# Two 512-token tiles of two batch rows, interleaved through every layer of a two-layer hybrid block, with a byte ring of 1 MB weight units

## The chip, the cores and the metric

The kernel runs on all eight cores of one Trainium2 chip (two dies, cores 0 to 3 and 4 to 7). The cores do not communicate: each works on two of the sixteen batch rows, with its own copy of all weights in memory. The metric is the device time of the slowest core in microseconds (us), one launch, everything included: the cast of the f32 weights, the conditioning and the whole sequence.

Executions come in two states. In the fast one all eight cores agree within about 1% (13215.8 to 13330.1 us in the profile of the kernel before). In the slow one the cores of one die, sometimes of both, show a lower granted TensorE clock and the time is longer: in one slow run of experiment 1, cores 4 to 7 took 13351 to 13659 us at 0.84 to 0.85, cores 0 to 3 12495 to 12507 at 0.93.

## The reference, cut to what matters

Two layers; 2048 channels; each core has 2 rows of 2048 tokens, that is 8 tiles of 512 tokens.

```
for l in range(2):
    mod = silu(c) @ w_mod[l] + b_mod[l]                  # 2048 x 12288, once per batch row
    sh_m, sc_m, g_m, sh_f, sc_f, g_f = split(mod, 6)
    h = x * (1 + sc_m) + sh_m
    a, val, gate, z = split(h @ w_in[l])                 # 2048 -> 3584
    y = concat(pool(a),                                  # trailing means, carry 16 tokens
               silu(LN(depthwise_conv31(val * sigmoid(gate)))),   # carries 31 tokens
               u * (tril(w_sgu) @ LN(v)))                # u, v = split(gelu(z)), chunks of 128
    x = LN(alpha * x + g_m * (y @ w_out[l]))             # 2048 -> 2048
    h = x * (1 + sc_f) + sh_f
    x = LN(alpha * x + g_f * (relu(h @ w_ff1[l])**2 @ w_ff2[l]))  # 2048 -> 8192 -> 2048
```

What matters: nothing in a tile can go on across an LN until the LN is done, and a tile needs only the tail of the tile before it *in the same row* (16 tokens for pooling, 31 for the convolution). Two tiles of different rows are independent.

## The kernel before

The activations are kept with channels on partitions, so an LN sums over partitions. TensorE does that with a matrix of ones. Weights arrive in slots of 2.1 MB (128 partitions x 8192 bf16), three slots deep. The first tile casts each slot from f32 on GpSimd's queue and stores the bf16 copy back to memory; later tiles read the copy.

```python
def w_issue():
    ...
    rb_ = WR[i % 3]
    if i < NSLOT * len(layers):                       # first tile
        k.dma("pool", rb_.v(BF16), wsl_d[rows, :], [], [rb_.reg], ...)      # cast
        k.dma("sp", wbfull_d[rows, :], rb_.v(BF16), [rb_.reg], [R_slot[g]], ...)  # store, if nt > 1
    else:
        k.dma("sp", rb_.v(BF16), wbfull_d[rows, :], [R_slot[g]], [rb_.reg], ...)
```

The modulation matrix is loaded whole (48 slots) before any tile starts:

```python
for grp in range(NGC // 4):                           # 48 times, 2.1 MB each
    k.dma("pool", wb_.v(BF16), wmod_d[grp * 128:(grp + 1) * 128, :], ...)   # cast
    for kc in range(KC):
        ... nc.tensor.matmul(bank[0:2, :], lhsT=c2v[:, kc, :], rhs=wv[:, kc * 512:(kc + 1) * 512], ...)
```

After each output chunk, GpSimd makes a bf16 copy and a bf16 square, and TensorE adds both up over partitions. After the last chunk the norm runs as one block:

```python
def resid_evac(l, b, gidx, oc, bank, bankr, pend):
    ... vector.scalar_tensor_tensor(out=xT[:, oc, :], in0=bank, scalar=gate, in1=xT[:, oc, :], ...)
    ... gpsimd.tensor_copy(out=rb[:, i, :], in_=xT[:, oc, :])
    ... gpsimd.tensor_tensor(out=rsq[:, i, :], in0=xT[:, oc, :], in1=xT[:, oc, :], op=ALU.mult)
    def stats():
        ... tensor.matmul(banks[SUMB], lhsT=oneb, rhs=rb[:, i, :], start=(oc == 0), stop=(oc == KC - 1))
        ... tensor.matmul(banks[SQB], lhsT=oneb, rhs=rsq[:, i, :], start=(oc == 0), stop=(oc == KC - 1))
    ...

def main_ln(...):
    ...                                               # flush stats, then mean and 1/std
    for kc in range(KC):
        ...                                           # VectorE: subtract mean; multiply by 1/std
        ...                                           # ScalarE: h chunk for the next stage; new x chunk
```

The stages of one tile follow one another in program order, one tile after the other:

```python
for ti in range(nt):                                  # 8 tiles
    ...                                               # load x, transpose on TensorE
    for li, l in enumerate(layers):
        ...                                           # input projection, conv, gating, output, norm,
        ...                                           # first MLP matmul, second, norm
    ...                                               # transpose, store y
```

The convolution multiplies by 31 diagonal matrices per 128 channels, which GpSimd builds anew for each tile and layer.

Of the kernel before, what the change touches and what calls it, by code (L numbers as in the profile page):

```python
# [19 lines left out]
NSLOT = 44  # L20
SLOTE = 8192
# [4 lines left out]
NGC = 192  # L26

# [28 lines left out]
class K:  # L56
    def __init__(self, nc, es):
        self.nc, self.es = nc, es
        self.eng = {}
        for name, h in (("pe", nc.tensor), ("act", nc.scalar), ("dve", nc.vector),  # L60
                        ("pool", nc.gpsimd), ("sp", nc.sync)):
            self.eng[name] = Eng(h, self.newsem("e_" + name), is_pe=(name == "pe"))
# [29 lines left out]
    def op(self, eng, fn, reads=(), writes=(), inc=True):  # L92
        E = self.eng[eng]
        self._waits(E, reads, writes)
        ins = fn()
        v = E.sem.count + 1
        if inc:
            ins.then_inc(E.sem.h, 1)
            E.sem.count += 1
        for R in reads:  # L100
            if R.r.get(E.sem, 0) < v:
                R.r[E.sem] = v
        for R in writes:
            R.w = (E.sem, v)
            R.r = {}
        return ins

    def dma(self, q, out, in_, reads, writes, sem, **kw):
        E = self.eng[q]
# [9 lines left out]
        return ins  # L119

# [18 lines left out]
def build_program(nt, layers, stop_after=None):  # L139
    n_cores, gather = 1, False  # L140
    nc = bass.Bass("TRN2", target_bir_lowering=False)
    ntok = nt * T
    nloc_slots = (L_ALL * NSLOT) // n_cores
    nloc_gc = NGC // n_cores
    nloc_grp = nloc_gc // 4
# [3 lines left out]
    x_d = dram("x", [ntok, D], F32, "ExternalInput")  # L149
    y_d = dram("y", [ntok, D], F32, "ExternalOutput")  # L150
    wsl_d = dram("wsl", [nloc_slots * 128, SLOTE], F32, "ExternalInput")
    wmod_d = dram("wmod", [NGC // 4 * 128, 8192], F32, "ExternalInput")
    bmod_d = dram("bmod", [128, NGC], F32, "ExternalInput")
    c2_d = dram("c2", [128, 32], F32, "ExternalInput")
    NPP = L_ALL * (6 * 31 + 6 * 3 + 4 + 16 * 4)
    pp_d = dram("pp", [128, NPP], F32, "ExternalInput")
    sgb_d = dram("sgb", [1, L_ALL * 2 * 768], F32, "ExternalInput")
    bsr_d = dram("bsr", [1, L_ALL * 6 * 128], F32, "ExternalInput")
    wp_d = dram("wp", [128, L_ALL * 4 * 128], F32, "ExternalInput")
    wst_d = dram("wst", [128, L_ALL * 6 * 128], F32, "ExternalInput")  # L160
    wbfull_d = dram("wbfull", [L_ALL * NSLOT * 128, SLOTE], BF16, "Internal")
    wbsh_d = wbfull_d
# [3 lines left out]
    with es:  # L166
        k = K(nc, es)
        ARENA = 212800
        arena_t = es.enter_context(nc.sbuf_tensor("arena", [128, ARENA], U8))
        arena = arena_t[:, :]  # L170
        psum_t = es.enter_context(nc.psum_tensor("ps", [128, 8 * 512], F32))
        psum = psum_t[:, :]
        banks = [psum[:, i * 512:(i + 1) * 512] for i in range(8)]
        bank_r = [Region("ps", i * 2048, (i + 1) * 2048, f"bank{i}") for i in range(8)]
        rr = [0]

        def nextbank():
            i = rr[0] % 6
            rr[0] += 1
            return banks[i], bank_r[i]  # L180
        SUMB, SQB = 6, 7

        cur = [0]

        def alloc(name, nbytes, at=None):
            if at is None:
                lo = (cur[0] + 63) // 64 * 64
                cur[0] = lo + nbytes
                assert cur[0] <= ARENA, (name, cur[0])
            else:  # L190
                lo = at
            return Buf(arena, lo, nbytes, name)

        XT = alloc("xT", 32768)
        HT = alloc("hT", 16384)
        U0 = (cur[0] + 63) // 64 * 64
        cur[0] = U0 + 65536
        WR = [alloc(f"wr{i}", 16384) for i in range(3)]
# [7 lines left out]
        YT = ualloc("yT", 16384)  # L206
        AT = ualloc("aT", 4 * 528 * 4)
        HC = ualloc("hcT", 6 * 544 * 2)
        CV = ualloc("cvT", 6 * 512 * 2)
        UT = ualloc("uT", 6 * 512 * 2)  # L210
        VLN = ualloc("vln", 4 * 768 * 2)
        VG = ualloc("vg", 768 * 4)
        PT = ualloc("ptmp", 2 * 528 * 4)
        DG = ualloc("diag", 31 * 128 * 2)
        H1 = Buf(arena, U0, 65536, "h1T")
        DG2 = Buf(arena, AT.lo, 31 * 128 * 2, "diag2")
        STG = [Buf(arena, U0 + i * 8192, 8192, f"stg{i}") for i in range(2)]
        WMB = [Buf(arena, U0 + i * 16384, 16384, f"wmb{i}") for i in range(4)]
        MF = Buf(arena, XT.lo, NGC * 16 * 4, "mf")
        WP32 = Buf(arena, XT.lo + 12288, L_ALL * 4 * 128 * 4, "wp32")  # L220
        WST32 = Buf(arena, XT.lo + 16384, L_ALL * 6 * 128 * 4, "wst32")
        ONESF = Buf(arena, XT.lo + 22528, 512, "onesf")
        IOTA = Buf(arena, XT.lo + 23040, 64, "iota")
        IOTF = Buf(arena, XT.lo + 23104, 64, "iotf")
        MSEL = Buf(arena, XT.lo + 23168, NGC * 16 * 4, "msel")
        RB = alloc("rb", 3 * 1024)
        RSQ = alloc("rsq", 3 * 1024)
        MEAN = alloc("mean", 2048)
        RSTD = alloc("rstd", 2048)
        TMPA = alloc("tmpa", 2048)  # L230
        FT = alloc("ft", 2 * 2048)
        SQT = alloc("sqt", 2 * 1024)
        ID32 = alloc("id32", 512)
        IDB = alloc("idb", 256)
        ONEB = alloc("oneb", 256)
        ONER = alloc("oner", 512)
        WMT = alloc("wmt", L_ALL * 6 * 128 * 2)
        WPB = alloc("wpb", L_ALL * 4 * 128 * 2)
        SGG = alloc("sgg", L_ALL * 768 * 4)
        SGBB = alloc("sgbb", L_ALL * 768 * 2)  # L240
        SGB32 = Buf(arena, XT.lo + 40960, L_ALL * 768 * 4, "sgb32")
        BSR = alloc("bsr", L_ALL * 6 * 128 * 4)
        PP = alloc("pp", NPP * 4)
        MOD2 = alloc("mod2", NGC * 2 * 4)
        DER = alloc("der", 9 * L_ALL * 32 * 4)
        INVC = alloc("invc", 4 * 16 * 4)
        AHALO = alloc("ahalo", L_ALL * 4 * 16 * 4)
        HHALO = alloc("hhalo", L_ALL * 6 * 32 * 2)
        SMALL = alloc("small", 256)
        CACT = Buf(arena, XT.lo + 36864, 256 * 4, "cact")  # L250
        SEL = Buf(arena, XT.lo + 39552, 32 * 4, "sel")
        EPSB = alloc("eps", 16)
        if nloc_gc <= 32:
            MODL = Buf(arena, XT.lo + 37888, nloc_gc * 16 * 4, "modl")
            BMOD = Buf(arena, XT.lo + 39424, nloc_gc * 4, "bmod")
        else:
            MODL = Buf(arena, WR[0].lo, NGC * 16 * 4, "modl")
            BMOD = Buf(arena, WR[1].lo, NGC * 4, "bmod")
# [3 lines left out]
        for nm, n in (("convw", 6 * 31), ("convb", 6), ("lncg", 6), ("lncb", 6), ("ls", 4),  # L262
                      ("lnmg", 16), ("lnmb", 16), ("lnfg", 16), ("lnfb", 16)):
            ppo[nm] = (o, n)
            o += L_ALL * n
        assert o == NPP

        def ppv(nm, l, i0=0, n=1):
            o, per = ppo[nm]
            a = o + l * per + i0  # L270
            return PP.v(F32)[:, a:a + n]

        csem = k.newsem("csem")
        castsem = k.newsem("castsem")
        gsem = k.newsem("gsem")
        msem = k.newsem("msem")
        wmsem = [k.newsem(f"wmsem{i}") for i in range(4)]
        ringsem = [k.newsem(f"ring{i}") for i in range(3)]
        stgsem = [k.newsem(f"stgs{i}") for i in range(2)]
        osem = [k.newsem(f"osem{i}") for i in range(2)]  # L280

        R_wbsh = Region("d_wbsh", 0, 1, "wbsh")
        R_wbfull = Region("d_wbfull", 0, 1, "wbfull") if gather else R_wbsh
        R_modsh = Region("d_modsh", 0, 1, "modsh")
        R_modfull = Region("d_modfull", 0, 1, "modfull") if gather else R_modsh
        R_y = Region("d_y", 0, 1, "y")

        C2 = Buf(arena, XT.lo + 36864, 32 * 4, "c2")
        BMD = Buf(arena, XT.lo + 37888, NGC * 4, "bmd")
        for buf, src in ((PP, pp_d), (C2, c2_d), (BMD, bmod_d), (WP32, wp_d), (WST32, wst_d)):  # L290
            k.dma("sp", buf.v(F32), src, [], [buf.reg], csem)
        k.dma("sp", BSR.v(F32), bsr_d.partition_broadcast(128), [], [BSR.reg], csem)
        k.dma("sp", SGG.v(F32), sgb_d[:, 0:L_ALL * 768].partition_broadcast(128), [], [SGG.reg], csem)
        k.dma("sp", SGB32.v(F32), sgb_d[:, L_ALL * 768:2 * L_ALL * 768].partition_broadcast(128), [], [SGB32.reg], csem)
        for b_ in (PP, C2, BMD, WP32, WST32, BSR, SGG, SGB32):
            b_.reg.w = (csem, csem.count)

        R_slot = {g: Region("d_wb", g, g + 1, f"wb{g}") for g in range(L_ALL * NSLOT)}
        stsem = [k.newsem(f"wst{i}") for i in range(3)]
        ringsem_sw = [k.newsem(f"ringsw{i}") for i in range(3)]  # L300

        k.op("dve", lambda: nc.vector.memset(EPSB.v(F32)[:, 0:1], EPS), [], [EPSB.reg])
        k.op("dve", lambda: nc.vector.memset(EPSB.v(F32)[:, 1:2], EPSM), [EPSB.reg], [EPSB.reg])
        k.op("pool", lambda: nc.gpsimd.memset(ONESF.v(F32), 1.0), [], [ONESF.reg])
        k.op("pool", lambda: nc.gpsimd.memset(ONEB.v(BF16), 1.0), [], [ONEB.reg])
        k.op("pool", lambda: nc.gpsimd.memset(ONER.v(F32), 1.0), [], [ONER.reg])
# [624 lines left out]
```

## Time and profile before

| | kernel before |
|---|---|
| median of three runs | 13378.98 us (13274.98 to 14025.92; the last is a slow run) |
| span in the profile | 13330.1 us |
| TensorE busy | 11420.8 us, 86% |
| VectorE, ScalarE, GpSimd busy | 21%, 17%, 12% |
| until the first tile starts | 770 us |
| first tile | 1870 us |
| a steady tile | 1518 us |

The last three rows come from the timeline and the table of windows. In all views of the profile PE is TensorE, PEld its weight loads, DVE VectorE, ACT ScalarE, POOL GpSimd and SP the engine that issues the plain weight transfers; L781 is line 781 of the kernel; `arena<-x` is a tile written from another. In a list of waits, `PE ps L550 <- DMA arena<-x` says that PE, at L550 and writing `ps`, waited for the DMA that writes `arena` from `x`. `ps` is TensorE's output memory, `arena` the one on-chip tensor that holds all buffers, `wsl` and `wmod` the f32 layer weights and modulation matrix, `wbfull` (`wb` in the new kernel) the bf16 copy of the weights in memory.

The page's chain of work that ended last, by engine, says the same in one line (shares of the span):

```profile
PE 74%; DMA 12%; DVE 6%; issue 5%; ACT 3%; POOL 0%; another core or an unknown queue 0%; DVEq 0%; ACTq 0%; SPq 0%; POOLq 0%
```

A quarter of the path is not TensorE: 12% are transfers (for the most part the modulation and the first tile), and 9% are VectorE and ScalarE, which come onto the path mainly in the norms and the modulation next to them, though each is busy for just a fifth of the time. The slices, the waits, the stage rows and the timeline across a norm stand in the prediction.

### The profile page before, as it was taken

To read this page: it belongs to the slowest core of one execution; us is meant where nothing else is said; L and a number is where in the kernel's file an instruction comes from. 1 tells how busy PE (TensorE), PEld (TensorE's weight loads), DVE (VectorE), ACT (ScalarE), POOL (GpSimd) and SP (SyncE) were. 2 spreads that over 40 slices of the span, in tenths; PEclk is the share of its full clock that TensorE was granted. 3 is DMA by queue.
4 is the path that set the end of the run, shared out by engine and by line. 5 is a ranking of instruction groups with operands and counts; after the bars stand their busy time and mean duration, and the time that the engine had idled before them with its cause. 6 is when DMAs were issued, how large, how long until landed. Compare 5 with 4: busy or idle time off the path is not lost.

```text
span 13330.1 us, 133467 instructions; the slowest of 8 cores (13215.8 to 13330.1 us)
## 1 busy us (share of the span) xinstructions
PE 11420.8 (86%) x51360; PEld 5122.7 (38%) x51360; DVE 2806.1 (21%) x4092; ACT 2329.1 (17%) x3346; POOL 1598.7 (12%) x1333
## 2 busy tenths in 40 slices
PE   3468878789898998989898898979898898979898
PEld 1133333334344443434344343434344343434433
DVE  0012031131312212131222212131221213122221
ACT  0011021120312212120212212031211212021220
POOL 0011120020201001020201101020100102020100
PEclk7679989899898999999999999989999999989987
DMA  8889989824243332334233232324233332433332
GB/s 138 141 187 199 215 191 209 201 111 149 96 151 126 127 139 108 137 116 150 104 144 140 108 139 108 145 108 152 108 139 139 112 135 110 149 114 139 120 120 101
DMA packets 184169, 1841.38 MB, mean 138 GB/s; under 512 B 14720, under 2 KB 14848, under 8 KB 85248
## 3 DMA queue, kind: packets, MB, share of 16 engines
q1 hardware_dynamic: 107136, 1514.06, 30.6%
q0 software_dynamic: 71808, 285.22, 13.5%
q10 hardware_dynamic: 4608, 33.56, 0.6%
q8 instruction: 426, 6.98, 0.2%
q14 instruction: 191, 1.56, 0.0%
HBM read 1899.89 MB, written 218.10 MB: 159 GB/s over the span
## 4 chain that ended last, share of the span: by engine, by line
PE 74%; DMA 12%; DVE 6%; issue 5%; ACT 3%; POOL 0%; another core or an unknown queue 0%; DVEq 0%; ACTq 0%; SPq 0%; POOLq 0%
PE ps L781 25%; PE ps L771 23%; PE ps L615 8%; PE ps L738 7%; DMA arena<-wsl 7%; PE ps L674 5%; DMA arena<-wmod 4%; DVE arena L504 3%; PE ps L578 2%; DMA y<-arena 1%; PE ps L340 1%; DMA arena<-x 1%; PE ps L528 1%; ACT arena L561 1%; PE ps L531 1%
## 5 line engine op out<-in xcount | busy, mean ns | idle before, releaser
L781 PE MATMUL ps<-arena 128*128 128x512 bf16 x16384 | 3662.9, 386 | 117.0 <-DMA arena<-wsl 117.0
L771 PE MATMUL ps<-arena 128*128 128x512 bf16 x15360 | 3376.3, 383 | 84.6 <-DMA arena<-wsl 84.6
L781 PEld LDWEIGHTS ps<-arena 128*128 128x128 bf16 x16384 | 1622.1, 99 | 2125.7 <-issue 345.0
L771 PEld LDWEIGHTS ps<-arena 128*128 128x128 bf16 x15360 | 1514.4, 99 | 1943.8 <-issue 206.5
L518 DVE SCALAR_TENSOR_TENSOR arena<-ps,arena 128x512 f32<-128x512 f32 x512 | 384.6, 751 | 4439.2 <-PE ps L781 3634.6
L747 DVE SCALAR_TENSOR_TENSOR arena<-ps,arena 128x512 bf16<-128x512 f32 x1024 | 705.6, 692 | 2865.2 <-ACT arena L745 2865.0
L738 PE MATMUL ps<-arena 128*128 128x512 bf16 x4096 | 1017.5, 397 | 314.5 <-ACT arena L724 231.1
L523 POOL CAST arena<-arena 128x512 bf16<-128x512 f32 x512 | 312.0, 609 | 8037.1 <-DVE arena L518 8037.1
L615 PE MATMUL ps<-arena 128*128 128x512 bf16 x5632 | 1233.2, 382 | 34.1 <-DMA arena<-wsl 34.1
L745 ACT ACTIVATE arena<-ps 128x512 f32<-128x512 f32 x1024 | 610.4, 598 | 2866.4 <-PE ps L771 2857.9
L615 PEld LDWEIGHTS ps<-arena 128*128 128x128 bf16 x5632 | 553.2, 98 | 709.7 <-issue 58.0
L738 PEld LDWEIGHTS ps<-arena 128*128 128x128 bf16 x4096 | 409.3, 100 | 881.4 <-issue 450.2
L668 POOL TENSOR_TENSOR arena<-arena 128x3968 bf16<-128x3968 bf16 x96 | 654.0, 6820 | 707.4 <-DVE arena L646 470.0
L494 ACT ACTIVATE arena<-arena 128x512 f32<-128x512 f32 x48 | 34.7, 723 | 3902.2 <-DVE arena L491 3901.8
L674 PE MATMUL ps<-arena 128*128 128x512 bf16 x2976 | 656.5, 379 | 0.0
L578 PE MATMUL ps<-arena 128*128 128x384 bf16 x2048 | 433.4, 358 | 239.0 <-ACT arena L510 202.3
L340 PE MATMUL ps<-arena 128*2 128x512 bf16 x768 | 270.9, 530 | 391.3 <-DMA arena<-wmod 391.3
L524 POOL TENSOR_TENSOR arena<-arena 128x512 bf16<-128x512 f32 x512 | 531.5, 1038 | 0.0
L760 PE MATMUL ps<-arena 128*128 128x512 bf16 x1024 | 285.8, 411 | 271.2 <-ACT arena L510 271.0
L513 ACT ACTIVATE arena<-arena 128x512 f32<-128x512 f32 x512 | 418.2, 817 | 145.1 <-DVE arena L507 109.3
L674 PEld LDWEIGHTS ps<-arena 128*128 128x128 bf16 x2976 | 290.0, 98 | 355.7 <-issue 7.7
L578 PEld LDWEIGHTS ps<-arena 128*128 128x128 bf16 x2048 | 210.0, 103 | 460.8 <-issue 354.8
(103 smaller groups left out, 4503.1 us busy)
## 6 DMA issues: line engine op xcount, KB each, us to landing
arena<-wbfull SPq DMA_DIRECT2D x616, 2048.0 KB, 7.8
arena<-wsl POOLq DMA_DIRECT2D x88, 2048.0 KB, 40.0
wbfull<-arena SPq DMA_DIRECT2D x88, 2048.0 KB, 14.8
arena<-wmod POOLq DMA_DIRECT2D x48, 2048.0 KB, 34.1
arena<-x SPq DMA_DIRECT2D x32, 1024.0 KB, 4.9
y<-arena ACTq DMA_DIRECT2D x32, 1024.0 KB, 4.3
arena<-sgb SPq DMA_DIRECT2D x2, 768.0 KB, 14.8
arena<-wst SPq DMA_DIRECT2D x1, 768.0 KB, 9.4
```

Of the source, the lines that this page charges most:

```text
L340: k.op("pe", lambda kc=kc, wv=wv, bank=bank: nc.tensor.matmul(bank[0:2, :], lhsT=c2v[:, kc, :], rhs=wv[:, kc * 512:(kc + 1) * 512], start= ...
L513: k.op("act", lambda kc=kc: nc.scalar.activation(out=xT[:, kc, :], in_=xT[:, kc, :], func=AF.Identity, scale=ppv(gname, l, kc), bias=ppv(b ...
L524: k.op("pool", lambda: nc.gpsimd.tensor_tensor(out=rsq[:, i, :], in0=xT[:, oc, :], in1=xT[:, oc, :], op=ALU.mult), [xr(oc)], [rsr])
L578: k.op("pe", lambda kc=kc, wv=wv, bank=bank, tb=tb: nc.tensor.matmul(bank[:, 0:384], lhsT=hT[:, kc, tb * 128:(tb + 1) * 128], rhs=wv[:, kc ...
L615: k.op("pe", lambda kc=kc, e0=e0, wv=wv, bank=bank: nc.tensor.matmul(bank, lhsT=wv[:, e0:e0 + 128], rhs=hT[:, kc, :], start=(kc == 0), sto ...
L668: k.op("pool", lambda c=c, diag=diag: nc.gpsimd.tensor_tensor(out=diag, in0=idb.unsqueeze(1).to_broadcast([128, 31, 128]), in1=ppv("convw" ...
L674: k.op("pe", lambda c=c, kk=kk, bank=bank, diag=diag: nc.tensor.matmul(bank, lhsT=diag[:, kk, :], rhs=hcT[:, c, 32 - kk:544 - kk], start=( ...
L738: k.op("pe", lambda kc=kc, ki=ki, e0=e0, wv=wv, bank=bank: nc.tensor.matmul(bank, lhsT=wv[:, e0:e0 + 128], rhs=yT[:, kc, :], start=(ki == ...
L745: k.op("act", lambda: nc.scalar.activation(out=ft[:, j % 2, :], in_=bank, func=AF.Square), [bankr], [fr])
L747: k.op("dve", lambda: nc.vector.scalar_tensor_tensor(out=h1T[:, j, :], in0=bank, scalar=0.0, in1=ft[:, j % 2, :], op0=ALU.is_gt, op1=ALU.m ...
L771: k.op("pe", lambda kc=kc, e0=e0, wv=wv, bank=bank: nc.tensor.matmul(bank, lhsT=wv[:, e0:e0 + 128], rhs=hT[:, kc, :], start=(kc == 0), sto ...
L781: k.op("pe", lambda j=j, wv=wv, bank=bank: nc.tensor.matmul(bank, lhsT=wv[:, j * 128:(j + 1) * 128], rhs=h1T[:, j, :], start=(j == 0), sto ...
```

## The change

The intent: give TensorE work of another tile while one tile's norm runs, and spread the modulation matrix over the first pair's stages. The tiles of the two batch rows form a pair, and a pair goes through each stage as A, B, with everything that is not the stage's own matmuls placed between its steps as background items. Buffers had to shrink for a second tile's x: weights come in units of 1.05 MB (128 x 4096 bf16) in a ring of 40960 bytes per partition (five units). The core of the diff (cuts marked):

```diff
-NSLOT = 44
-SLOTE = 8192
+UE = 4096
+RING = 40960
...
+class Bg:
+    def pump(self, i):
+        want = len(self.items) * (i + 1 - self.s0) / float(self.s1 - self.s0)
+        while self.done < len(self.items) and self.done < want:
+            self.items[self.done]()
+            self.done += 1
...
-    nc = bass.Bass("TRN2", target_bir_lowering=False)
+    nc = bass.Bass("TRN2", target_bir_lowering=False, dynamic_dma_scratch_size=4096)
-        ARENA = 212800
+        ARENA = 225088
-        XT = alloc("xT", 32768)
+        X = [alloc("xA", 32768), alloc("xB", 32768)]
-        WR = [alloc(f"wr{i}", 16384) for i in range(3)]
+        RG = alloc("ring", RING)
...
+        def ring_fill():
+            while ring["issued"] < len(order):
+                ...                                   # next unit's bytes lo .. lo + n
+                if any(a < lo + n and lo < b_ for _, a, b_ in ring["live"]):
+                    return
+                ...                                   # cast, cast + store, or read, as before
...
 # statistics (in resid)
-            k.op("pool", lambda: nc.gpsimd.tensor_copy(out=rb[:, i, :], in_=xT[:, oc, :]), [xr(oc)], [rbr])
-            k.op("pool", lambda: nc.gpsimd.tensor_tensor(out=rsq[:, i, :], ..., op=ALU.mult), ...)
-            ...                                       # two bf16 matmuls with ones per chunk
+            k.op("act", lambda: nc.scalar.activation(out=sq[i], in_=xT[b][:, oc, :], func=AF.Square), ...)
+            k.op("pool", lambda: nc.gpsimd.tensor_tensor(out=acc, in0=p0, in1=xT[b][:, oc, :], op=ALU.add), ...)
+            k.op("pool", lambda: nc.gpsimd.tensor_tensor(out=acq, in0=q0, in1=sq[i], op=ALU.add), ...)
+            # two f32 matmuls with ones per norm, in ln_stats_items
...
 # schedule
-        for ti in range(nt):
-            ...
+            for u in range(16):
+                mod_unit(u)                           # 16 of 96 modulation units first
+            ...
+                    bgs = [Bg(pool_items(1, l, first), 7, 20), Bg(conv_ln_items(0, l, SQ, sq), 0, 7)]
+                    if start:
+                        bgs.append(Bg(mod_items(range(16, 40)), 0, 17))
+                    run(in_steps(1, l, first), bgs)
+                    ...
+                    run(out_steps(0, l), [Bg(conv_ln_items(1, l, FT, ft), 0, 12)])
+                    bgs = [Bg(main_ln_items(0, l, "lnmg", "lnmb", h_items(0, l, S1F, SHF)), 0, 15)]
+                    ...
+                    run(out_steps(1, l), bgs)
+                    run(ff1_steps(0, l), [Bg(main_ln_items(1, l, "lnmg", "lnmb"), 0, 50)])
+                    run(ff2_steps(0, l), [Bg(h_items(1, l, S1F, SHF), 0, 32)])
+                    ...
+                    run(ff1_steps(1, l), bgs)         # A's second norm beside B's MLP
```

`run(steps, bgs)` issues one step (usually 16 matmuls), then as many background items as are due. Three smaller things go with it: the convolution's diagonal matrices are now six weight units a layer, made on the host; the gating unit's LN gain and bias are folded into one multiply-add after its matmul; and the modulation matmuls have the weights stationary, with two moving columns.

## The prediction

> **What bounds the kernel now.** I first read the busy shares and the slices of the page. TensorE (PE) is busy 11420.8 us of a 13330.1 us span; no other engine exceeds 21%. In the slices the first row is PE, the second the granted PE clock, the third the DMA engines:
>
> ```profile
> PE   3468878789898998989898898979898898979898
> PEclk7679989899898999999999999989999999989987
> DMA  8889989824243332334233232324233332433332
> ```
>
> There are three stages: two slices with PE near half idle (the modulation matrix is loaded), then about six with the DMA engines at 80 to 90% or more (the first tile, whose weights are cast from f32 and stored back as bf16), then a steady part with DMA at 20 to 40% and PE near full, with dips. Next I asked for what PE waits for (us in total, times, longest):
>
> ```profile
> PE ps L340 <- DMA arena<-wmod: 391.3, 48, 43.1
> PE ps L760 <- ACT arena L510: 271.0, 219, 10.0
> PE ps L738 <- ACT arena L724: 231.1, 80, 10.8
> PE ps L578 <- ACT arena L510: 202.3, 128, 8.4
> PE ps L793 <- ACT arena L513: 179.2, 128, 8.3
> PE ps L550 <- DMA arena<-x: 147.7, 29, 14.7
> PE ps L781 <- DMA arena<-wsl: 117.0, 32, 5.4
> PE ps L771 <- DMA arena<-wsl: 84.6, 22, 5.8
> ```
>
> The four rows on ACT are one thing: a layer norm stands between two matmul stages of the only tile there is, so PE waits for statistics, normalisation and the affine step. Then the stage table (busy us of each engine, then clock, DMA share, GB/s), one row for the first tile and one for a steady tile, and the timeline of PE around a norm and inside a dense stage:
>
> ```profile
> 770.00:2640.00 1870.00, 1472.41 (x6287) 641.86 (x6287) 352.99 (x523) 287.41 (x412) 249.78 (x233) 0.89 0.92 203
> 8718.00:10236.00 1518.00, 1364.42 (x6275) 618.35 (x6273) 348.47 (x503) 287.41 (x412) 186.60 (x148) 0.94 0.34 128
> ```
>
> ```profile
> 8220.11 207.36 PE L771 MATMUL ps<-arena 128*128 128x512 bf16 x960
> ...
> 9438.54 0.38 PE L531 MATMUL ps<-arena 128*128 128x512 bf16 x1 [0.62 <-POOL arena L524]
> 9447.21 0.48 PE L578 MATMUL ps<-arena 128*128 128x384 bf16 x1 [8.29 <-ACT arena L510]
> 9448.72 0.48 PE L578 MATMUL ps<-arena 128*128 128x384 bf16 x1 [1.03 <-ACT arena L510]
> ```
>
> The dense stage runs at 207.36/960 = 216 ns a matmul. Across the norm PE stands 8.29 us and then goes at the pace of the normalisation. So the steady part is bound by PE plus exposed norms, and the first tile by DMA.
>
> [...] the dense stretches have 1.00, a steady tile with its norms 0.94. [...] eight cores run the same dense stages at 1.00. [...] (core 1, then core 2, same stretch):
>
> ```profile
> 12960.00:13020.00 60.00, 60.00 (x230) 24.81 (x229) 7.61 (x11) 6.58 (x11) 0.00 (x0) 0.81 0.29 106
> 12960.00:13020.00 60.00, 60.00 (x280) 27.20 (x279) 12.16 (x18) 10.15 (x17) 0.00 (x0) 1.00 0.41 146
> ```
>
> [...] the f32 weights come on the POOL queue alone, the bf16 ones on SP's. [...]
>
> **Cost of a megabyte.** From the queue table:
>
> ```profile
> q1 hardware_dynamic: 107136, 1514.06, 30.6%
> q0 software_dynamic: 71808, 285.22, 13.5%
> ```
>
> q1: 0.306 x 13330 / 1514 = 2.7 us per MB of bf16. q0: 0.135 x 13330 / 285 = 6.3 us per MB delivered by a cast. A cast with its store, when that is all there is, from the first tile's timeline:
>
> ```profile
> 2470.93 15.66 PE L781 MATMUL ps<-arena 128*128 128x512 bf16 x64 [3.98 <-DMA arena<-wsl]
> 2490.75 15.66 PE L781 MATMUL ps<-arena 128*128 128x512 bf16 x64 [3.73 <-DMA arena<-wsl]
> ```
>
> 19.8 us for 2.1 MB, 9.4 us per MB. The modulation casts alone come four (8.4 MB) in 61 us: 7.3 us per MB.
>
> **The change, part by part.** PE work of one layer of one tile now: 512-wide matmuls 352 (input) + 4 + 186 (convolution) + 12 + 256 (output) + 2048 (MLP) + 64 (norm statistics) = 2922 at 216 ns = 631 us; 128 of 384 columns at 0.16 us = 21; together with the small ones about 653 us. Two layers and 128 transposes at about 0.15 us: 1325 us. The steady tile takes 1518, so about 193 us are lost to norms, x and y traffic and a cold clock.
>
> *Statistics.* The 64 statistics matmuls (13.8 us) go; VectorE, ScalarE and GpSimd sum over channels, and 4 f32 matmuls remain [...]. New minimum about 642 us per layer and tile. GpSimd adds twice per output chunk, 2 x 1.04 us (the row of L524), within the 3.45 us that 16 matmuls take; ScalarE and VectorE also stay below a step's time. The convolution's diagonal matrices no longer cost GpSimd 654 us; they come as 6 more units a layer.
>
> *Interleaving.* Each norm, modulation, x load and y store of one tile is now placed between matmul steps of the other. A pair has four layer-tiles: 4 x 642 = 2569, plus 256 transposes 36, plus what I leave exposed: about 20 for x and y staging (one buffer, and the x loads queue behind weight loads on SP), about 12 per layer where a norm's end and the next stage meet (24), and 10 for clock dips. 2660 us a pair against 3036 now, 376 less, three times: 7980 us. Weights are still read for each tile: 96.5 MB a layer x 2.7 = 260 us of DMA beside 642 of PE, so hidden.
>
> *First pair.* Tile A casts and stores, tile B reads back, and 80 of 96 modulation units (84 MB) now travel with layer 0. By stage, max of PE and DMA. Layer 0: input A 14.7 MB x 9.4 = 137; convolution A 59; input B 97 PE + 46 for modulation matmuls, against 40 + 25 MB x 7 = 216 of DMA, so 216; convolution B 41; output 78 and 81; MLP A twice 33.5 x 9.4 = 313; MLP B twice 270. Sum 1778. Layer 1, without modulation: 137 + 59 + 97 + 41 + 78 + 56 + 313 + 313 + 221 + 221 = 1536. Together 3314; five units of prefetch carry some slack from PE-bound into DMA-bound stages, so I take 3250. Modulation matmuls: 32 a unit at 62 ns (24 small ones took 1.50 us), 2 us, 96 times.
>
> *Start and end.* Now PE gets the first x at 766 us. Then only 16 modulation units come first: 16.8 MB x 7.3 = 123, plus x and constants: 150. The last tile's norm and store stay exposed: 50.
>
> Sum: 150 + 3250 + 7980 + 50 = **11430 us**. Against today's 13330: start 770 to 150, first two tiles 1870 + 1518 to 3250, three pairs 9108 to 7980.
>
> **The rivals.** *The clock becomes the bound.* With no dips PE runs dense for milliseconds, where now 440 us is the longest stretch. [...] For it: those rows, and one of three runs 5% slower. Against it: 1.00 in every other dense stage of all cores. I give lasting throttling 5 to 10%, occasional throttling (up to 700 us) another 20%.
>
> *DMA holds the first pair longer.* [...] stores on SP wait for casts, and reads and x loads stand behind them; a cast on POOL waits for PE and the store, and the norm sums stand behind it. The ring is 5 MB where it was 6, and z units cut it. If casts reach only 80% of today's rate, the first pair costs 500 more: 11900. Against it: the first tile now keeps the DMA engines at 0.92 with a similar depth.
>
> *The norm is only moved.* If the GpSimd sums lag, or ScalarE's table switches pile up, PE waits at each new statistics matmul; 5 us at 28 places would add 140. *Transfers are not the steady bound*: a share of 0.34 speaks against it.
>
> **Range and chances.** I add 90 for some throttling to 11430: 11520. Low side, 11200: more slack carried, or stalls nearly nil. High side, 12150: a throttled stretch, or slow casts with some throttling. Only lasting throttling brings it near 13379.
>
> **What would show it.** Modulation waits ahead of the first input matmul down from about 770 to about 150 us; the first pair ending near 3400, DMA share near 0.9 in it and PE waiting for wsl; a steady pair near 2660 with clock 0.98 or more and the waits on the norm's ACT rows nearly gone; statistics matmuls waiting under 2 us. Wrong would be: 0.81 over whole slices, DMA waits in the steady pairs, or GpSimd ahead of PE.

**What the sum came to.** The sum, 150 + 3250 + 7980 + 50 = 11430 us, contains two things:

- *The f32 statistics matmuls*, four per layer and tile, at 0.9 us each: 3.6 of the 642 us, 14 of a pair's 2660, 43 of the 7980. The trace before has no f32 matmul of 512 columns, so nothing there showed the figure. In the kernel after, two of them take 0.86 us inside a dense stretch (L558, 5056.93 to 5057.79 us), 0.43 each.
- *The allowances*: 20 for x and y, 24 for the norms' ends, 10 for clock dips, 54 in each pair; so too the 90 for throttling that were added to the sum. They are worked out from no trace.

On the clock, the two rows in the prediction are what the trace shows: from 12960 to 13020 us, in a dense stage, core 1 stands at 0.81 and core 2 at 1.00; core 0 also has 0.81 there, cores 3 to 7 1.00. What sets the granted clock is not shown. At the 0.81 of that row the 7980 would be 7980 / 0.81 = 9850 and the whole about 13300 us (an estimate from the row), no gain. On the queues, the trace before has SP waiting 1753 us, in 87 waits, for a cast to land before it issues the store, and GpSimd waiting 133 us, in 8, for a store before it issues the next cast. All 88 + 48 casts of layer weights and modulation are GpSimd's issues, and the 616 reads of the bf16 copy are SP's. ScalarE loads its tables 209 times there, 1.28 us each.

## The result, and the profile after

| | before | after |
|---|---|---|
| all runs, us | 13378.98, 14025.92, 13274.98, 14631.45 | 11279.17, 11271.61, 11273.11, 11279.99 |
| median | 13702.45 | 11276.14 |
| fast runs | 2 of 4 | 4 of 4 |
| instructions | 133467 | 138033 |

The ratio of the fast runs is 0.8481, with a 95% interval from 0.8449 to 0.8513: the changed kernel takes 15% less. (The plain ratio of the means of the fast runs in the table is 0.8461, within that interval. The medians are not compared, as the one before has two slow runs in it.) All outputs agreed with the reference.

The page's busy line, its slices and its chain, of the kernel after:

```profile
PE 10653.8 (94%) x52392; PEld 4950.3 (44%) x52392; DVE 2691.0 (24%) x4061; ACT 2406.3 (21%) x3626; POOL 1457.2 (13%) x1381
...
PE   4687799997999999999999999999999999999998
...
PEclk7899999999999999999999999999999999999999
DMA  9999999799644444444444444444445444434443
...
PE 80%; DMA 18%; issue 1%; DVE 0%; ACT 0%; POOL 0%; SPq 0%; POOLq 0%; ACTq 0%; DVEq 0%
```

Beside the slices that the prediction shows, two things have changed. The dips of the steady part are gone: from the eleventh slice on PE stands at 9 in all but the last. And the DMA-bound stretch is still there, about ten slices of 282 us. VectorE and ScalarE were 9% of the path and are now nothing; DMA has risen from 12% to 18% of it. By the page's lines the casts of the weights went from 7% to 10% and their stores came to 3%, while the modulation went from 4% to 3% of a shorter span: in the first pair more of the path is now the weights.

The stage table of core 2 (span of the stage, then busy us of PE, PEld, DVE, ACT and POOL, then clock, DMA share, GB/s): layer 0 of the first pair, layer 1 of it, the second pair.

```profile
141.00:1899.00 1758.00, 1446.86 (x8658) 674.17 (x8657) 322.71 (x560) 283.98 (x426) 277.33 (x306) 0.93 0.97 216
1899.00:3406.00 1507.00, 1357.90 (x6171) 611.97 (x6170) 337.80 (x507) 301.58 (x454) 223.03 (x229) 0.96 0.79 201
3406.00:6018.00 2612.00, 2603.42 (x12330) 1211.09 (x12329) 666.91 (x977) 600.45 (x906) 312.34 (x272) 1.00 0.43 155
```

A steady pair is 2612, 2608 and 2602 us, with PE busy all but some 8 us of it and the clock at 1.00. Before, two steady tiles took 2 x 1518 = 3036 us. In layer 0 of the first pair the DMA engines are at 0.97: that stage is a transfer. In layer 1 they are at 0.79 and PE is busy 90%: neither is full. Here something could still be had, and an experiment below takes it.

What PE waits for between 3130 and 11200 us, that is from shortly before the second pair to 28 us before the end of the last (us in total, times, longest), complete:

```profile
PE ps L515 <- DMA arena<-x: 9.8, 3, 4.0
PE ps L558 <- POOL arena L852: 7.2, 3, 2.4
PE ps L782 <- ACT arena L768: 3.8, 12, 0.6
PE ps L785 <- ACT arena L771: 2.4, 12, 0.2
```

23 us in three pairs. Before, the four rows on ScalarE alone came to 884 us over the run. L515 is the transpose of x, L558 the f32 statistics matmul, L782 and L785 the convolution's statistics. The wait for GpSimd's sums (L852) is 2.4 us and comes once a pair.

### The profile page after: what moved, and what is told of

It reads as the page before. It is cut to its first block, busy times and chain, and to the rows that moved or that the text cites. A ratio compares the mean times of both kernels' runs of the same rounds, so it can differ in the third digit from the quotient of the medians.

```text
span 11277.8 us, 138033 instructions; the slowest of 8 cores (11238.2 to 11277.8 us)
## 1 busy us (share of the span) xinstructions
PE 10653.8 (94%) x52392; PEld 4950.3 (44%) x52392; DVE 2691.0 (24%) x4061; ACT 2406.3 (21%) x3626; POOL 1457.2 (13%) x1381
## 4 chain that ended last, share of the span: by engine, by line
PE 80%; DMA 18%; issue 1%; DVE 0%; ACT 0%; POOL 0%; SPq 0%; POOLq 0%; ACTq 0%; DVEq 0%
PE ps L402 37%; PE ps L915 26%; DMA arena<-wsl 10%; PE ps L871 7%; PE ps L764 5%; DMA arena<-wmod 3%; DMA wb<-arena 3%; PE ps L668 2%; DMA arena<-x 1%; PE ps L515 1%; DMA arena<-wz 0%; PE ps L486 0%; PE ps L540 0%; DMA arena<-wb 0%; DMA y<-arena 0%
## 5 line engine op out<-in xcount | busy, mean ns | idle before, releaser
L402 PE MATMUL ps<-arena 128*128 128x512 bf16 x22016 | 4849.3, 382 | 130.2 <-DMA arena<-wsl 95.7
L915 PE MATMUL ps<-arena 128*128 128x512 bf16 x16384 | 3608.5, 382 | 135.2 <-DMA arena<-wsl 129.0
L402 PEld LDWEIGHTS ps<-arena 128*128 128x128 bf16 x22016 | 2162.3, 99 | 2777.6 <-issue 258.3
L915 PEld LDWEIGHTS ps<-arena 128*128 128x128 bf16 x16384 | 1606.0, 98 | 2080.6 <-issue 215.0
L852 POOL TENSOR_TENSOR arena<-arena 128x512 f32<-128x512 f32 x480 | 609.7, 1270 | 6124.2 <-DVE arena L840 6123.0
L840 DVE SCALAR_TENSOR_TENSOR arena<-ps,arena 128x512 f32<-128x512 f32 x512 | 383.3, 749 | 3666.4 <-PE ps L915 3259.2
L844 ACT ACTIVATE arena<-arena 128x512 f32<-128x512 f32 x512 | 321.9, 629 | 3659.6 <-DVE arena L840 3659.5
L871 PE MATMUL ps<-arena 128*128 128x512 bf16 x4096 | 891.5, 380 | 14.3 <-DMA arena<-wb 11.4
L764 PE MATMUL ps<-arena 128*128 128x512 bf16 x2976 | 664.2, 382 | 19.1 <-DMA arena<-wsl 18.2
L871 PEld LDWEIGHTS ps<-arena 128*128 128x128 bf16 x4096 | 400.3, 98 | 500.5 <-issue 24.2
L854 POOL TENSOR_TENSOR arena<-arena 128x512 f32<-128x512 f32 x480 | 608.0, 1267 | 1.1
L592 ACT ACTIVATE arena<-arena 128x512 f32<-128x512 f32 x512 | 415.1, 811 | 837.2 <-DVE arena L587 820.1
L764 PEld LDWEIGHTS ps<-arena 128*128 128x128 bf16 x2976 | 291.2, 98 | 364.8 <-issue 28.6
L603 ACT ACTIVATE arena<-arena 128x512 bf16<-128x512 f32 x512 | 394.5, 803 | 114.3 <-DVE arena L493 106.8
L668 PE MATMUL ps<-arena 128*128 128x384 bf16 x2048 | 351.2, 333 | 21.1 <-DMA arena<-wz 16.4
L587 DVE TENSOR_TENSOR arena<-ps,arena 128x512 f32<-128x512 f32 x512 | 354.4, 692 | 54.2 <-DVE arena L584 0.9
L584 DVE SCALAR_TENSOR_TENSOR arena<-ps,arena 128x512 f32<-128x512 f32 x512 | 348.6, 681 | 0.0
L123 POOL DMA_DIRECT2D arena<-wsl x178 | 128.2, 721 | 1341.3 <-DMA wb<-arena 922.7
L668 PEld LDWEIGHTS ps<-arena 128*128 128x128 bf16 x2048 | 203.4, 100 | 162.0 <-issue 36.6
L799 DVE SCALAR_TENSOR_TENSOR arena<-ps,arena 128x512 f32<-128x512 f32 x96 | 72.1, 751 | 794.3 <-PE ps L794 794.3
```

Of the source, the lines that this page charges most:

```text
L402: k.op("pe", lambda kc=kc: nc.tensor.matmul(bank, lhsT=wv[:, e0 + kc * 128:e0 + kc * 128 + 128], rhs=rhs(kc), start=(kc == 0), stop=(kc == ...
L592: k.op("act", lambda: nc.scalar.activation(out=xT[b][:, kc, :], in_=xT[b][:, kc, :], func=AF.Identity, scale=ppv(gname, l, kc), bias=ppv(b ...
L603: k.op("act", lambda: nc.scalar.activation(out=hT[:, kc, :], in_=xT[b][:, kc, :], func=AF.Identity, scale=dsc(msc, l, kc, b), bias=dsc(msh ...
L668: k.op("pe", lambda kc=kc, wv=wv: nc.tensor.matmul(bank[:, 0:384], lhsT=hT[:, kc, tb * 128:(tb + 1) * 128], rhs=wv[:, (kc % 8) * 384:(kc % ...
L764: k.op("pe", lambda kk=kk: nc.tensor.matmul(bank, lhsT=wv[:, kk * 128:(kk + 1) * 128], rhs=hcT[:, c, 32 - kk:544 - kk], start=(kk == 0), s ...
L840: k.op("dve", lambda: nc.vector.scalar_tensor_tensor(out=xT[b][:, oc, :], in0=bank, scalar=dsc(gm, l, oc, b), in1=xT[b][:, oc, :], op0=ALU ...
```

## The experiments

The first seven kernels ran on one chip, the last two on another. On both the kernel before was fast in 1 of 7, 1 of 7 and 2 of 11 runs, and its slow ones took 14.1 to 15.2 ms. Its fast runs there were 13257.91, 13269.22, 13275.22 and 13261.84 us. So most verdicts below rest on one or two fast runs of a kernel, and I compare them with the fast 11276 and 13270. The changed kernel itself was not run again in these rounds. The kernel before shows how far fast runs can differ: 13258 to 13275 us here, 13275 and 13379 in the first comparison, 0.9% in all. All outputs were correct.

**The theory.** The gain has three large parts: norms, x and y traffic hidden behind the other tile's matmuls; modulation hidden in a stage that DMA bounds anyway; and fewer matmuls and a deep enough ring to keep both true. **Rivals**: the gain comes from the other edits (statistics, diagonals, buffers) and the order matters little; PE is not really the bound in the steady part, so that PE work put back would cost nothing; the ring or the smaller reserve (`dynamic_dma_scratch_size=4096`) holds the first pair up.

### 1. Take the overlap away

The background items are no longer spread, but issued in one piece at the end of the stage that carried them. Everything else, each instruction included, stays.

```diff
     def pump(self, i):
+        return
         want = len(self.items) * (i + 1 - self.s0) / float(self.s1 - self.s0)
```

> The changed kernel, with the norm, modulation, x and y work no longer placed between the matmul steps but in one piece after each stage (same instructions, other order). Theory (the steady pairs gain because this work now lies beside the other tile's matmuls): PE waits again at about five places per layer: the norm and modulation ahead of the first MLP stage (some 35 us), two modulations of 13 us, the convolution norm ahead of the second output stage (12 us), the pool sums and norms that the next statistics wait for (20 to 30 us), and about 60 us of x and y work per pair; a steady pair goes from 2608 to about 2870 us, the whole to 12000 to 12300. Rival (the order hardly matters, because the engines' queues run ahead and two tiles are enough; the gain is the shorter start and the cheaper statistics): under 150 us more, below 11430.

Measured: one fast run of six, the profiled one, 12510.48 us, 11% over the changed kernel. (That is 210 us above the expected range: the pair came out as expected, but the loss in the first pair was larger.) The second pair, and what PE waits for between 3830 and 12440 us, the first rows (line numbers are one higher than in the kernel after):

```profile
3830.00:6714.00 2884.00, 2669.18 (x12095) 1221.44 (x12328) 670.88 (x977) 609.05 (x906) 312.42 (x272) 0.95 0.39 140
```

```profile
PE ps L403 <- ACT arena L604: 147.5, 172, 2.7
PE ps L516 <- DMA arena<-x: 89.9, 17, 14.1
PE ps L872 <- ACT arena L833: 87.3, 30, 11.2
```

The pair took 2884 us (the next 2885) against 2612 and 2608. The extra 272 to 277 us fall in two parts: PE busy is 2669 and not 2603, 66 us, which goes with a mean clock of 0.95 in place of 1.00 for the same matmuls, now that the holes are back (in the kernel before the trace shows this on the spot: a clock of 0.50 from 9448 to 9460 us, right after the hole of 8.29 us that the prediction shows); the rest, some 206 us, is idle. The waits are the old ones: ScalarE's affine step (L604), its activation after the convolution's norm (L833) and x. By stages the whole run lost 424 us up to the end of the first pair, 272 and 277 in the next two and 258 in the last with the tail: 1231. So the placing alone is worth about 1230 of the 2050 us. The rival that the other edits bring most of it falls. This run still goes through the stages as A, B; what that alternation alone is worth, without the placing, is not separated from the other edits.

### 2. Do all modulation first

```diff
-            for u in range(16):
+            for u in range(96):
                 mod_unit(u)
...
-                    if start:
-                        bgs.append(Bg(mod_items(range(16, 40)), 0, 17))
```

(and the three other groups of modulation items in the same way)

> The changed kernel with all 96 modulation units ahead of the first tile, as the kernel before has them, instead of 16 ahead and 80 spread over layer 0. Theory (each stage of layer 0 takes the larger of its PE and its DMA time, as the prediction summed them): the start grows by 80 x 6.15 us = 490, layer 0 of the first pair shrinks from 1758 to about 1520, so about 11530 in all. Rival A (the first pair is bound by the sum of its DMA work, so moving units within it changes nothing): 11280. Rival B (the units were free in layer 0): 11770.

Measured: one fast run of four, the profiled one, 11544.12 us. The start and layer 0 of the first pair, on core 4:

```profile
0.00:645.00 645.00, 114.62 (x3144) 105.73 (x3146) 30.71 (x134) 12.89 (x18) 77.53 (x112) 1.00 1.02 171
645.00:2161.00 1516.00, 1343.05 (x5978) 604.94 (x6094) 310.50 (x475) 278.82 (x419) 220.21 (x226) 0.95 0.79 196
```

The start grew by 504 us (645 for 141) and layer 0 shrank by 242 (1516 for 1758). The net, +262 by stages and +268 by the totals, is what spreading the modulation is worth. It isn't the whole 504, as a stage that DMA bounds still has to carry the units; about half of the 80 units' time was free. Both rivals fall: that the place of the units changes nothing, and that they were free in layer 0.

### 3. Put PE work back

Two matmuls with ones per output chunk, whose results nothing reads, stand in for the bf16 statistics that the change removed.

```diff
+            xb, xbr = nextbank()
+            for r_ in range(2):
+                k.op("pe", lambda: nc.tensor.matmul(xb, lhsT=oneb, rhs=WMT.v(BF16)[:, 0:512], ...
             i = oc % 2
```

> The changed kernel with the PE work of the old statistics put back as idle work: two extra 128x512 bf16 matmuls into a spare bank after each output chunk, 64 per layer and tile, 1024 in all. Theory (the steady pairs are bound by PE alone, at 0.216 us a matmul): 12 of 16 layer-tiles and tile B of the first pair pay in full, tile A of the first pair hides it behind its DMA: 14/16 x 221 = 193 us more, 11470. Rival (something beside PE paces the steps, the vector engines or the loads): under 60 us more.

Measured: one fast run of six, 11453.29 us, +177. The profile fell in a slow run, but its die 1 was undisturbed (cores 4 to 7: 11442.0 to 11453.8 us, clock 0.978 to 0.980). Where the first matmul of L668 (part of the input projection, so a fixed point of a pair) stands in the third and the fourth pair, in the timeline of the kernel after and then of this one's core 4:

```profile
6078.46 2.76 PE L668 MATMUL ps<-arena 128*128 128x384 bf16 x16
...
8686.50 2.76 PE L668 MATMUL ps<-arena 128*128 128x384 bf16 x16
```

```profile
6135.86 2.76 PE L668 MATMUL ps<-arena 128*128 128x384 bf16 x16
...
8798.06 2.76 PE L668 MATMUL ps<-arena 128*128 128x384 bf16 x16
```

A pair takes 2662 us for 2608: +54, against 256 x 0.216 = 55. In the steady part all PE work counts in full, so PE is the bound there. By the same point of the second pair only 9 us had been lost (3475.85 for 3466.95): the first pair hides most of its 55. The expectation had taken 14 of 16 parts as exposed; a first pair bound by DMA hides more than that.

### 4. A shallower ring, and 5. the same ring with the default reserve

The first takes three units instead of five. The second takes the same ring and leaves out `dynamic_dma_scratch_size=4096`, with the arena back at 212800 bytes per partition as in the kernel before: the 12288 bytes that the changed kernel has as ring are then neither ring nor arena. What the reserve holds no trace shows; only its effect on the time is tried.

```diff
-RING = 40960
+RING = 28672
```

```diff
-RING = 40960
+RING = 28672
...
-    nc = bass.Bass("TRN2", target_bir_lowering=False, dynamic_dma_scratch_size=4096)
+    nc = bass.Bass("TRN2", target_bir_lowering=False)
-        ARENA = 225088
+        ARENA = 212800
```

> The changed kernel with a weight ring of 28672 bytes per partition instead of 40960, [...] the reserve stays at 4096. Theory (depth is spare in the steady pairs, where DMA is busy 43%, except around the four held z units, which leave no room for the next unit; in the first pair fewer casts are in flight): steady pairs 20 to 40 us longer each, first pair 100 to 250 longer, 11450 to 11650. Rival (one unit ahead is enough everywhere): within 50 us of 11276.

> The same ring of 28672 bytes [...]. [...] equal to the run with the small reserve within 0.3% in fast runs. Rival (the small reserve holds casts back): the first pair is 100 us or more shorter here than there.

Measured: 11664.86 and 11665.17 us for the first, 11659.61 and 11669.72 for the second (two fast runs of four each). They are the same within 0.05%, so with a ring of three units the reserve of 4096 bytes cost nothing (with five, where more casts can be under way, it was not tried), and the space as ring is worth 389 us, 3.4%. Most of it is lost in the first pair, 3588 us for 3265; I had expected 100 to 250 and it was 323, which put the whole 15 us above the expected range. The steady pairs lose about 20 us each (2629, 2632). The stretch from 141 to 1899 us of the first of the two kernels, for comparison with layer 0 above:

```profile
141.00:1899.00 1758.00, 1334.21 (x7256) 599.11 (x7256) 312.97 (x535) 273.37 (x409) 237.62 (x267) 0.87 0.86 190
```

The DMA share is 0.86 and not 0.97, and PE got through 7256 matmuls instead of 8658. So the shallow ring leaves both less busy. One reading is that a stage bound by PE blocks the next casts, as no place in the ring is free, and PE then waits in the stage after it; only with enough depth does a stage take the larger of its PE and DMA time, as the prediction's sum assumed. The traces bear this out only in part. GpSimd, which issues the casts (L123), waited in the first pair 1306 us, in 155 waits, for a store out of the ring to land, against 1005 us in 120 waits with five units; its waits for PE at that line came to 977 against 909 us. So it is mostly the stores, and less PE, that the casts wait longer for; what makes the first pair longer is not settled beyond that.

### 6. The new statistics alone, in the kernel before

Only the statistics of the two norms move to ScalarE, GpSimd and two f32 matmuls; nothing is interleaved.

```diff
-            k.op("pool", lambda: nc.gpsimd.tensor_copy(out=rb[:, i, :], in_=xT[:, oc, :]), [xr(oc)], [rbr])
...
+            k.op("act", lambda: nc.scalar.activation(out=sq[i], in_=xT[:, oc, :], func=AF.Square), ...)
...
+            k.op("pool", lambda: nc.gpsimd.tensor_tensor(out=acc, in0=p0, in1=xT[:, oc, :], op=ALU.add), ...)
+            k.op("pool", lambda: nc.gpsimd.tensor_tensor(out=acq, in0=q0, in1=sq[i], op=ALU.add), ...)
```

> The kernel before with one part of the change alone: the norm's statistics summed by ScalarE and GpSimd in f32 and reduced by two f32 matmuls, instead of 32 bf16 matmuls per norm; no interleaving. Theory (PE is the bound between norms, and the norm's chain is exposed): 60 fewer matmuls per layer and tile save 13 us, 2 x 2 f32 matmuls cost 2 us, the chain at each norm grows by 1 to 2 us of GpSimd and f32 matmul time: 16 x 8 = 130 us less, a ratio of 0.990 to before. Rival (the statistics were hidden, or the longer chain eats the gain): 0.997 to 1.005.

> The same kernel as the statistics alone before, since only one of its six runs was fast: fast runs near 13160 us and a ratio near 0.992 to the fast runs of before, 0.997 to 1.005 if that one was luck.

Measured: 13163.97 us in the one fast run of the first round of runs, 13158.02 and 13148.50 in the second. The ratio to the kernel before of the second is 0.9913 (0.987 to 0.9956): some 115 us, 0.9%, under the 2% that would be called faster (the record's verdict is "unclear"), but the interval excludes 1. A shorter PE path is partly repaid as a longer wait at the norm, since the f32 sum of the last chunk must be there first. The row in what PE waits for (core 1 of this kernel; a slow run's profile, whose core was on the less disturbed die):

```profile
PE ps L536 <- POOL arena L530: 77.1, 32, 2.4
```

32 norms, 2.4 us each, where the rows for the bf16 statistics had 32.3 and 18.0 us in all. In the interleaved kernel the same wait comes three times in the last three pairs, so the same edit can earn more there: experiment 3 lost 177 us when the matmuls came back.

### 7. A version that beats both

In layer 1 of the first pair, tile A casts and stores (9.4 us per MB, bound by DMA), and tile B reads the copy back (2.7 us per MB, bound by PE). Casting twice costs about as much transfer time as casting, storing and reading once: 2 x 5.9 = 11.8 for 12.1. (5.9 us per MB is the pace of ten modulation casts of 1.05 MB in the kernel after, from 71.59 to 132.96 us.) But it is even: 33.5 MB of an MLP stage at 5.9 are 198 us, under the 221 of PE, for both tiles. The store is put off: 10% of the units are stored when tile A of the first pair visits them, 25% at its tile B, 55% and 10% at tiles A and B of the second pair, which has DMA time to spare. Until its store a unit is cast anew at each visit.

```diff
+VISIT = (3, 2, 3, 3, 1, 3, 2, 3, 4, 3, 2, 3, 3, 1, 3, 2, 3, 4, 3, 2)
...
+                        visits[(kind, g)] = visits.get((kind, g), 0) + 1
                         k.dma("pool", buf.v(BF16), f_d[rows, :], [], [buf.reg], ringsw[s], max_dma_last_dim=8192)
+                        if visits[(kind, g)] < store_visit(kind, g):     # 1 in layer 0, VISIT in layer 1
+                            ...                                           # keep the unit, no store yet
+                            continue
```

> An attempt to beat both: the weights of layer 1 are cast again on their first visits and stored at visit 1, 2, 3 or 4 (10, 25, 55 and 10% of the units), so that no visit carries cast and store of everything. Theory (tile A of the first pair is bound by the bytes of cast plus store, 9.4 us per MB, and a cast alone at 6.3 us per MB just fits under PE's 6.6): layer 1 of the first pair goes from 1507 to about 1330 and the second pair loses at most 50, so 11100 to 11180. Rival (casts are bound by their own queue, by its latency of 18 to 36 us and five units of ring, not by bytes): tile A hardly gains, tile B and the second pair lose 200 to 300 us, 11450 or more.

> The same kernel as the deferred stores before, since only one of its four runs was fast: a fast run between 11140 and 11170 us if that one was sound, against 11270 to 11280 for the changed kernel; near 11276 if it was luck.

Measured: 11154.30 us (one fast run of four), then 11144.55 and 11147.54 (two of six) on the other chip; the mean is 11149, about 1.1% below 11276. The two kernels were not timed in one round; but six of the eight cores of the profiled run end below 11150 where none of the kernel after's does below 11230 (11238.2 to 11277.8 us in its profile), and the gain stands in the stage that was meant. Layer 1 of the first pair and the second pair, core 3:

```profile
1899.00:3245.00 1346.00, 1306.51 (x6155) 606.04 (x6154) 337.36 (x506) 301.11 (x453) 278.49 (x307) 0.98 0.95 179
3245.00:5892.00 2647.00, 2610.27 (x12329) 1210.96 (x12327) 666.73 (x976) 602.42 (x906) 361.85 (x339) 1.00 0.59 176
```

Layer 1 went from 1507 to 1346 us and PE is busy 97% of it; the second pair paid 35 us of the 161 back (2647 for 2612, with the DMA share up from 0.43 to 0.59), the other two nothing. The stages of the second chip's run are the same (1346 and 2647 us).

## Why the prediction was right

The prediction was 11520 us with a sum of 11430; the result is 11276. It was right in direction, range and mechanism, though near the low end of its range (11200). Its steps against the stage table:

| step | predicted, us | measured, us |
|---|---|---|
| start | 150 | 141 |
| first pair | 3250 | 3265 |
| its layer 0 / layer 1, before the allowance for prefetch | 1778 / 1536 | 1758 / 1507 |
| three steady pairs | 7980 | 7822 |
| tail | 50 | 50 |
| sum | 11430 | 11278 |
| allowance for throttling | 90 | 0 |

**The mechanism.** "The steady part is bound by PE plus exposed norms, and the first tile by DMA" was right: experiment 1 puts the norms back and the pair grows by 272 to 277 us; experiment 3 adds PE work and the pair grows by all of it.

**The term that was mis-sized** is "what I leave exposed" in the pair: 20 for x and y, 24 for norms' ends, 10 for clock dips, 54 in all over a PE minimum of 2605. Measured is nearly nothing: pairs of 2602 to 2612, 23 us of waits in three pairs, the clock at 1.00. That is 158 us, as much as the 152 by which the whole sum was off. Some 8 us a pair of it lie in the minimum itself: 256 transposes were put at 36 us, and at 0.11 us each they are 28. The timeline near the end of the first pair shows it:

```profile
3165.39 3.62 PE L915 MATMUL ps<-arena 128*128 128x512 bf16 x16
3168.84 0.60 PE L540 MATMUL ps<-arena 128*128 128x128 f32 x4
3169.28 3.62 PE L915 MATMUL ps<-arena 128*128 128x512 bf16 x16
```

From one dense step to the next are 3.89 us where 16 matmuls take 3.45, so four transposes cost 0.44. The second column is the time to the end of the last one, which overlaps the next step, and must not be added up.

**First pair.** Adding up the larger of PE and DMA per stage held within 2% for each layer; the 64 us taken off for prefetch across stages were too many by 15. Two wrong sizes hid in it. Modulation matmuls were put at 2 us a unit, by the duration of matmuls with 128 columns; with two columns a unit of 32 takes 0.99 us. And a modulation unit was put at 7.3 us per MB; the units come at a pitch of 6.3 us for 1.05 MB, 6.0 us per MB:

```profile
78.06 0.99 PE L486 MATMUL ps<-arena 128*128 128x2 bf16 x32 [5.48 <-DMA arena<-wmod]
84.32 0.99 PE L486 MATMUL ps<-arena 128*128 128x2 bf16 x32 [5.27 <-DMA arena<-wmod]
```

The slower rate was that of the kernel before, whose modulation slots came four at a time with a gap of about 18 us after each four, and not the transfer's own. Some stages took longer than their sums, such as layer 0's input of tile A (160 us for 137), and some less, such as the output projections (142 for 159 in layer 0, 112 for 134 in layer 1). The four MLP stages of layer 0 took 1126 us for 1166. None of these changed what bounds a stage; but that the pair came within 15 us, while its stages, or groups of them, were off by up to 40, is partly luck: the errors cancel.

**Statistics.** "Twice per output chunk, 2 x 1.04 us" was too low. The row taken was a multiply with a bf16 result; the new sum has two f32 inputs and an f32 result; whether the operation or the type makes the difference the runs don't tell. The rows of the kernel after and of the one before, from the groups of instructions:

```profile
L852 POOL TENSOR_TENSOR arena<-arena 128x512 f32<-128x512 f32 x480 | 609.7, 1270 | 6124.2 <-DVE arena L840 6123.0
```

```profile
L524 POOL TENSOR_TENSOR arena<-arena 128x512 bf16<-128x512 f32 x512 | 531.5, 1038 | 0.0
```

1.27 us each, 2.54 per chunk. It still fits into a step of 3.45 us, so the conclusion stood: GpSimd idles 6124 us before L852, waiting for VectorE's next chunk. VectorE (L840, 0.75 us a chunk) and ScalarE (L844, 0.63 us) are below a step's time too, as predicted.

**The rivals.** *Lasting throttling* did not come in the fast runs: 1.00 on dense pairs for 7.8 ms. The prediction under-rated how often a chip is in the slow state, though; on the two chips of the experiments most runs of all kernels together, the one before included, were in it. Nothing shows that the density of the new kernel brings it: there the kernel before was slow in 21 of 25 runs, and the densely interleaved kernels (experiments 2 to 5 and 7) in 19 of 28. *DMA holds the first pair longer* came in part with a ring of three units (3588 us, experiment 4), and not with five. *The norm is only moved*: three waits of 2.4 us instead of 28 of 5; only the sign "under 2 us" was missed; ScalarE's table loads, which it named, went from 209 to 89, at 1.28 us each; and x, 9.8 us in three pairs, is the one DMA wait that the steady pairs have.

**Where the time went.** Start 770 to 141, -629; first two tiles 1870 + 1518 to 3265, -123, although 80 modulation units moved in; six steady tiles 9108 to 7822, -1286; the tail 64 to 50: together -2052. Of the 429 us per steady pair (3036 to 2608), 272 to 277 are the placing, by experiment 1. The statistics are some 29 by experiment 6 (115 over four pairs), or up to 54 by experiment 3. The remaining 100 to 125, from the diagonals that GpSimd no longer builds, the second buffers, the folded gain and the alternation of A and B as such, were not tried one by one and stay open.

## What to carry to other kernels

If an engine at 86% shows its idle time as many short waits on normalisation, look for an independent second piece of work and put one's norm between the other's matmul steps; here that alone was worth about 1230 of 2050 us, a quarter of which, in a steady pair, was the lower clock that went with the holes. Predict each stage as the larger of its engine time and its transfer time, and give prefetch enough depth for that to hold: two units fewer cost 3.4%. Where two neighbouring stages are bound by different things, move transfers from one to the other, even if they are not fewer: a store put off by a pair gave another 1.1%.
